# Layer 1's queries and forward forget gates, projected for pairs of heads ahead of the head loop by seven quarter products

## The chip, the cores and the metric

The kernel runs on one NeuronCore of a Trainium2 chip. The core has TensorE (PE, matmuls into PSUM banks; PEld are its weight loads), VectorE (DVE), ScalarE (ACT), GpSimd (POOL) and SyncE (SP, which here only issues DMAs), and 16 DMA engines between DRAM and SBUF. The metric is the device time of one execution in microseconds, taken as the median of several runs.

## The reference

Two layers work on 1024 latent tokens (`LAT`) and 256 context tokens (`CTX`) of width 1024. Layer 0 (attention and mLSTM heads) is not touched. Layer 1 has 16 heads of a gated linear recurrence that runs forward and backward:

```python
q, f_fwd, f_bwd, i, z = _split_cols(h @ w_in, C_SIZES)      # five blocks of 2048 columns
f = lb + (1.0 - lb) * jax.nn.sigmoid(f_pre.astype(F32))     # for each direction
k, lf, q = 1.0 - f, jnp.log(f), jax.nn.silu(q)
# per chunk: b = cumsum(lf);  S = exp(bL) * S + (k * exp(bL - b))^T v;  o = (q * exp(b)) S + ...
```

Each head takes 128 columns of each block. The queries are wanted for the latent tokens, the two forget gates `f_fwd` and `f_bwd` for latent and context tokens, the values `i` for both, the output gate `z` for the latent ones. The head outputs are normalised, multiplied by `silu(z)` and go through an output projection.

## The kernel before

The activations of layer 1 lie in SBUF transposed, as `hh + hl`: a value rounded to the matmul's 32-bit type and the rest. Weights are split the same way on arrival (`split`, L73 on ACT and L74 on DVE). `dense` (L131 to L133) makes each product from three matmuls, high by high, high by low, low by high, over k-blocks of 128 rows; a full projection of 128 columns has 8 k-blocks, so 24 matmuls for each group of up to 512 tokens.

Layer 1 handles the 16 heads one after the other, in this order of emission. `hg_proj` projects the forget gates of both directions (three token groups each: 256, 512, 512; sigmoid at L988, scaling at L989) into the tile `gF`, and the queries (two groups of 512, L997 and L998) into `gq`. `hg_intra` makes `k = 1 - f` (`gK`, L1061), two sums `gkn` (L1068), `Q = q * f` (`gQ`, L1070) and a first set of small matmuls ("strips", L1091), and then runs seven levels (`hg_level`): a copy of selected keys (`gksel`, L1121, ACT), 16 pairs of strips on PE, and on DVE `gQ` and `gK` times the decay (L1138), a masked copy (L1144) and the next level's decay (L1142). A level writes over the `gQ` that its strips read. `hg_vz` projects values and output gates (`wz` weights, 216 matmuls of 256 columns, outputs `gv` and `gz`). `hg_close` transposes `gK` (L1103, copies L1105), `hg_ctx` makes the state that the context leaves (L1043, L1045, L1050, L1052), `hg_scan` carries states backward (L1158, L1160) and forward (L1174, L1176) over 8 chunks and sums the output (L1169 to L1171). Then `hg_proj` of the next head is emitted, and the finished head goes out to DRAM.

The order on each engine is set by a planner that walks through the emitted instructions with its own idea of durations: an instruction that is ready and was emitted earlier goes first, the strips and the levels before all else (`urgent`). Each engine then works through its fixed order, and a semaphore holds an instruction whose inputs are late. `gQ`, `gK`, `gA`, `gz` and the `wz` weights have one buffer each; `gq` and `gv` have two; `gF` alternates between two pools from head to head. PSUM has two banks for projections (`mm`), two for transposes (`tr`), and three for strips and states (`s`). The next head's projections need neither this head's `gQ` nor its `gK`, so that they can lie anywhere in this head. After head 15 comes the output projection, whose first product is filled in during that head.

The lines that the change touches in `build` are these:

```python
wf = [self.wring([a["wc"][:, 2048 : 2048 + P]], P), None]   # weights of head 0, while layer 0 ends
st = self.hg_proj(0, pool, wf)
for h in range(16):
    hv = self.hg_intra(h, st, pool)
    self.hg_vz(h, st, pool)
```

## Time and profile before

| What | Value |
|---|---|
| Median of 3 runs | 3349.77 us (3348.98 to 3350.4) |
| Profiled execution, first to last instruction | 3349.2 us; its own time is not listed, the median lies 0.6 us above this span |
| PE busy in the span | 3316.9 us (99%) |
| DVE, ACT, POOL busy | 2028.9, 1401.3, 659.4 us (61%, 42%, 20%) |
| First key tile of a head (L1061) | head 0 at 1820.8 us, head 15 at 3120.3 us |
| Moved by DMA | 342.02 MB, mean 102 GB/s |

An engine's busy time is the union of its instructions. Matmuls overlap one another, and their ends are modelled, so that the time of a matmul in a stream is better read from the distance between two starts than from its duration. In a list of instructions in order of time, a bracket gives the idle time of the engine before the instruction, and what ended it. In a list of windows, each engine has its busy microseconds and the number of its instructions.

### The profile page before, as it was taken

The numbers are of one execution on the slowest core, as the hardware profiler recorded it, in microseconds if no ns is written. First come the engines' busy times: TensorE is split into PE (matmuls) and PEld (weight loads), VectorE is DVE, ScalarE is ACT, GpSimd is POOL, SyncE is SP. The second block draws the span as 40 slices with busy tenths as digits, with TensorE's granted clock in tenths as the row PEclk, the third lists the DMA queues.
The fourth block names the chain that finished last, engine by engine and source line by source line (L and its number), as shares of the span: only waits on it lengthen the run. The fifth ranks groups of instructions, "written<-read, shape, count | busy, mean of one in ns | idle before, by whom it ended". The sixth has DMA issues, their size and how long they took to land. (4 is left out here: it accounts for less than half of the span.)

```text
span 3349.2 us, 64282 instructions
## 1 busy us (share of the span) xinstructions
PE 3316.9 (99%) x25006; PEld 2940.9 (88%) x25006; DVE 2028.9 (61%) x4785; ACT 1401.3 (42%) x3301; POOL 659.4 (20%) x1059
## 2 busy tenths in 40 slices
PE   7999999999999999999999999999999999999999
PEld 6699899988989888898888999999999999999887
DVE  5337666666655466787666555555555555555657
ACT  5335554455443444454454333333333333333343
POOL 2222222212211111221110112121211222321110
PEclk9999999999999999999999999999999999999999
DMA  7713222232233444444653122211222222222267
GB/s 247 242 51 84 85 72 81 67 92 84 77 90 96 150 125 122 136 134 139 213 174 91 45 68 69 70 61 61 67 64 67 73 64 58 73 77 58 76 176 204
DMA packets 322992, 342.02 MB, mean 102 GB/s; under 512 B 32296, under 2 KB 265448, under 8 KB 321664
## 3 DMA queue, kind: packets, MB, share of 16 engines
q1 hardware_dynamic: 276816, 217.85, 22.3%
q0 software_dynamic: 45872, 120.07, 11.8%
q8 instruction: 197, 3.23, 0.4%
q14 instruction: 107, 0.88, 0.1%
HBM read 253.43 MB, written 84.21 MB: 101 GB/s over the span
## 5 line engine op out<-in xcount | busy, mean ns | idle before, releaser
L131 PE MATMUL mm<-hh,wh 128*128 128x512 f32 (+1 forms) x1600 | 585.4, 366 | 0.6 <-ACT gF L988 0.6
L132 PE MATMUL mm<-hl,wh 128*128 128x512 f32 (+1 forms) x1600 | 584.5, 365 | 0.0
L133 PE MATMUL mm<-hh,wl 128*128 128x512 f32 (+1 forms) x1600 | 580.6, 363 | 0.0
L131 PE MATMUL mm<-wh,hh 128*128 128x256 f32 (+1 forms) x1440 | 445.9, 310 | 1.7 <-DVE graw L1368 0.8
L132 PE MATMUL mm<-wl,hh 128*128 128x256 f32 (+1 forms) x1440 | 444.7, 309 | 0.0
L133 PE MATMUL mm<-wh,hl 128*128 128x256 f32 (+1 forms) x1440 | 442.0, 307 | 0.0
L131 PEld LDWEIGHTS mm<-hh,wh 128*128 128x128 f32 x1600 | 301.5, 188 | 47.6 <-ACT ev L371 4.2
L133 PEld LDWEIGHTS mm<-hh,wl 128*128 128x128 f32 x1600 | 301.5, 188 | 43.6 <-issue 0.2
L132 PEld LDWEIGHTS mm<-hl,wh 128*128 128x128 f32 x1600 | 301.7, 189 | 40.5 <-issue 0.2
L133 PE MATMUL mm<-wzh,hl 128*128 128x256 f32 x1024 | 291.6, 285 | 0.0
L132 PE MATMUL mm<-wzl,hh 128*128 128x256 f32 x1024 | 291.6, 285 | 0.0
L131 PE MATMUL mm<-wzh,hh 128*128 128x256 f32 x1024 | 291.3, 284 | 0.0
L131 PEld LDWEIGHTS mm<-wh,hh 128*128 128x128 f32 x1440 | 271.3, 188 | 20.7 <-ACT ev L352 3.4
L132 PEld LDWEIGHTS mm<-wl,hh 128*128 128x128 f32 x1440 | 271.4, 188 | 12.8 <-issue 0.7
L133 PEld LDWEIGHTS mm<-wh,hl 128*128 128x128 f32 x1440 | 271.3, 188 | 12.0 <-issue 0.5
L74 DVE TENSOR_TENSOR wl<-wraw,wh 128x512 fp32r<-128x512 f32 x240 | 165.8, 696 | 129.7 <-ACT wh L73 126.5
L73 ACT CAST wh<-wraw 128x512 fp32r<-128x512 f32 x240 | 147.2, 619 | 230.9 <-PE mm L132 181.6
L1121 ACT COPY gksel<-gK 128x1024 f32<-128x1024 f32 x96 | 111.0, 1156 | 224.5 <-PE s L1091 154.5
L132 PEld LDWEIGHTS mm<-wzl,hh 128*128 128x128 f32 x1024 | 193.5, 189 | 2.5
L131 PEld LDWEIGHTS mm<-wzh,hh 128*128 128x128 f32 x1024 | 193.2, 189 | 2.6
L133 PEld LDWEIGHTS mm<-wzh,hl 128*128 128x128 f32 x1024 | 193.3, 189 | 1.6
L1138 DVE TENSOR_TENSOR gQ<-gQ,gF 128x1024 f32<-128x1024 f32 x112 | 138.1, 1233 | 77.9 <-PE s L1091 77.9
(488 smaller groups left out, 7414.9 us busy)
## 6 DMA issues: line engine op xcount, KB each, us to landing
wraw<-in_wab_dram SPq DMA_DIRECT2D x108, 256.0 KB
wraw<-in_wc_dram SPq DMA_DIRECT2D x96, 256.0 KB
wraw<-yd SPq DMA_DIRECT2D x92, 256.0 KB
wraw<-in_wc_dram SPq DMA_DIRECT2D x128, 128.0 KB
md<-ev POOLq DMA_DIRECT2D x60, 256.0 KB, 2.7
mloz<-md SPq DMA_DIRECT2D x40, 256.0 KB
s<-gyt POOLq DMA_DIRECT2D x36, 256.0 KB, 4.4
adar<-in_wada_dram SPq DMA_DIRECT2D x16, 512.0 KB
```

The lines of the kernel that those rows point to most:

```text
L73: m = nc.scalar.copy(hi, x)
L74: nc.vector.tensor_tensor(out=lo, in0=x, in1=hi.bitcast(F32), op=ALU.subtract)
L131: mm(ps, lhsT=lh(k), rhs=rh(k), start=(start and k == 0), stop=False)
L132: mm(ps, lhsT=lh(k), rhs=rl(k), start=False, stop=False)
L133: m = mm(ps, lhsT=ll(k), rhs=rh(k), start=False, stop=(stop and k == nk - 1))
L1121: m = nc.scalar.copy(ksel.rearrange("p (b s i) -> p b s i", s=2, i=h), pick(K))
L1138: nc.vector.tensor_tensor(out=v, in0=v, in1=tot, op=ALU.mult)
```

## The change

`hg_f` keeps from the old `hg_proj` only the backward forget gate of a head. Queries and forward forget gates are made for all heads by `hg_wide`, which runs after layer 0 and after `hg_f` of head 0, and before the pool of the head loop is opened. It takes 16 units, queries and gates in turn for each pair of heads. A unit sees `h` (1024 tokens by 1024 features) and its 256 columns of W as two by two quarters of 512 tokens by 512 features and of 512 features by 128 columns, and makes the two by two result from seven products of quarters. `half_sums` makes four sums of quarters of `h` once; `raws` loads four weight quarters per unit and makes four differences on POOL. Each product has 4 k-blocks, so 12 matmuls of 512 columns. Partial sums are combined in PSUM and by DVE; results go through sigmoid and scaling as before, and to the DRAM scratches `qd` and `fd`. The gates' context tokens (`cpart`) have the same matmuls as before, with half of the k-blocks at a time. `hg_proj` now loads a head's queries and forward gates from DRAM with four DMAs on SP. The value and output-gate weights of head 0 are loaded at the end of `hg_wide`.

```diff
-    def dense(self, ps, lh, ll, rh, rl, nk, start=True, stop=True):
+    def dense(self, ps, lh, ll, rh, rl, nk, start=True, stop=True, skip=False):
...
-    def hg_proj(self, h, pool, w=None):
+    def hg_f(self, h, pool, w=None):
         nc, a = self.nc, self.a
-        st = {}
-        col = lambda i: a["wc"][:, i * 2048 + h * P : i * 2048 + (h + 1) * P]
+        c0 = 2 * 2048 + h * P
         lb, olb = self.lb[:, 0, h : h + 1], self.lb[:, 1, h : h + 1]
         fp = pool if h % 2 else self.fp
         F = self.t(fp, [P, 2, LAT], F32, "gF", 1)
         Fc = self.t(fp, [P, 2, CTX], F32, "gFc", 1)
-        todo = [(d, t0, n) for d in range(2) for t0, n in ((LAT, CTX), (512, 512), (0, 512))]
-        if w:
-
-            todo.sort(key=lambda x: x[1] == 0)
-        w = w or [None, None]
-        for d, t0, n in todo:
-            w[d] = w[d] or self.wring([col(1 + d)], P)
+        w = w or self.wring([a["wc"][:, c0 : c0 + P]], P)
+        for t0, n in ((LAT, CTX), (512, 512), (0, 512)):
             ps = self.ps("mm", [P, n])
-            self.proj_tr(ps, w[d], 0, t0, n)
-            dst = Fc[:, d, :] if t0 == LAT else F[:, d, t0 : t0 + 512]
+            self.proj_tr(ps, w, 0, t0, n)
+            dst = Fc[:, 1, :] if t0 == LAT else F[:, 1, t0 : t0 + 512]
             nc.scalar.activation(dst, ps, AF.Sigmoid)
             nc.vector.tensor_scalar(out=dst, in0=dst, scalar1=olb, scalar2=lb, op0=ALU.mult, op1=ALU.add)
+        return F, Fc
+    def hg_proj(self, h, pool, FF=None):
+        dma = self.nc.sync.dma_start
+        F, Fc = FF or self.hg_f(h, pool)
+        dma(out=F[:, 0, :], in_=self.fd[h, :, 0:LAT])
+        dma(out=Fc[:, 0, :], in_=self.fd[h, :, LAT:T])
         q = {}
-        w = self.wring([col(0)], P)
-        for t0 in (512, 0):
-            ps = self.ps("mm", [P, 512])
-            self.proj_tr(ps, w, 0, t0, 512)
-            q[t0 // 512] = self.t(pool, [P, 512], F32, "gq", 2)
-            sg = self.t(pool, [P, 512], F32, "gsg", 1)
-            nc.scalar.activation(sg, ps, AF.Sigmoid)
-            nc.vector.tensor_tensor(out=q[t0 // 512], in0=sg, in1=ps, op=ALU.mult)
+        for hf in (1, 0):
+            q[hf] = self.t(pool, [P, 512], F32, "gq", 2)
+            dma(out=q[hf], in_=self.qd[h, :, hf * 512 : hf * 512 + 512])
         return dict(F=F, Fc=Fc, q=q)
 
+    def half_sums(self, pool, tp):
+        nc = self.nc
+        hh, hl = self.hh, self.hl
+        S = {n: [self.t(pool, [P, 4, 512], F32R, f"st{n}{c}", 1) for c in "hl"] for n in range(1, 5)}
+        def A(t, c, j):
+            s = slice(512 * t, 512 * t + 512)
+            return hh[:, 4 * c + j, s].bitcast(F32), hl[:, 4 * c + j, s].bitcast(F32)
+        def done(n, j, x):
+            self.split(S[n][0][:, j, :], S[n][1][:, j, :], x)
+        def pair(eng, out, x, y, op):
+            e = self.t(tp, [P, 512], F32, "br", self.brs)
+            eng.tensor_tensor(out=out, in0=x[0], in1=y[0], op=op)
+            eng.tensor_tensor(out=e, in0=x[1], in1=y[1], op=op)
+            eng.tensor_tensor(out=out, in0=out, in1=e, op=ALU.add)
+        tt = nc.vector.tensor_tensor
+        s1 = []
+        for j in range(4):
+            s1.append(self.t(tp, [P, 512], F32, "br", self.brs))
+            pair(nc.vector, s1[j], A(1, 0, j), A(1, 1, j), ALU.add)
+            done(1, j, s1[j])
+        s3 = []
+        for j in range(2):
+            s3.append(self.t(tp, [P, 512], F32, "br", self.brs))
+            pair(nc.gpsimd, s3[j], A(0, 0, j), A(1, 0, j), ALU.subtract)
+        for j in range(4):
+            for x in A(0, 0, j):
+                tt(out=s1[j], in0=s1[j], in1=x, op=ALU.subtract)
+            done(2, j, s1[j])
+        for j in range(4):
+            if j > 1:
+                s3.append(self.t(tp, [P, 512], F32, "br", self.brs))
+                pair(nc.gpsimd, s3[j], A(0, 0, j), A(1, 0, j), ALU.subtract)
+            done(3, j, s3[j])
+        for j in range(4):
+            h, l = A(0, 1, j)
+            tt(out=s1[j], in0=h, in1=s1[j], op=ALU.subtract)
+            tt(out=s1[j], in0=s1[j], in1=l, op=ALU.add)
+            done(4, j, s1[j])
+        return S
+    def hg_wide(self, sp, tp):
+        nc, a = self.nc, self.a
+        hh, hl = self.hh, self.hl
+        self.brs = 10
+        S = self.half_sums(sp, tp)
+        add = lambda out, x, y: nc.vector.tensor_tensor(out=out, in0=x, in1=y, op=ALU.add)
+        def X(n):
+            if isinstance(n, int):
+                return [lambda k, t=t: t[:, k, :] for t in S[n]]
+            t, c = n
+            return [lambda k, x=x: x[:, 4 * c + k, 512 * t : 512 * t + 512] for x in (hh, hl)]
+        def prod(ps, w, n, first):
+            x = X(n)
+            self.dense(ps, w.h, w.l, x[0], x[1], 4, first, True, True)
+        def raws(kind, i):
+            c0 = (2048 if kind == "f" else 0) + 2 * i * P
+            b = {}
+            for r, c in ((0, 0), (0, 1), (1, 1), (1, 0)):
+                b[(r, c)] = self.t(tp, [P, 512], F32, "br", self.brs)
+                nc.sync.dma_start(
+                    out=b[(r, c)].rearrange("p (k f) -> p k f", f=P),
+                    in_=a["wc"][r * 512 : r * 512 + 512, c0 + c * P : c0 + c * P + P].rearrange("(k p) f -> p k f", p=P),
+                )
+            def sub(x, y, out=None):
+                o = self.t(tp, [P, 512], F32, "br", self.brs) if out is None else out
+                nc.gpsimd.tensor_tensor(out=o, in0=x, in1=y, op=ALU.subtract)
+                return o
+            b["t1"] = sub(b[(0, 1)], b[(0, 0)])
+            b["t2"] = sub(b[(1, 1)], b["t1"])
+            b["t3"] = sub(b[(1, 1)], b[(0, 1)], None if kind == "f" else b[(0, 1)])
+            b["t4"] = sub(b[(1, 0)], b["t2"])
+            return b
+        units = [(kind, i) for i in range(8) for kind in "qf"]
+        order = lambda kind: [(0, 0), "t2", (1, 0), "t3", "t1", "t4"] + ([(0, 1)] if kind == "f" else []) + [(1, 1)]
+        queue = [(u, n) for u in range(len(units)) for n in order(units[u][0])]
+        rawd, forms = {}, {}
+        def more(n):
+            for u, f in queue[:n]:
+                if u not in rawd:
+                    rawd[u] = raws(*units[u])
+                hi, lo = [self.t(self.wp, [P, 512], F32R, "w" + c, self.slabs) for c in "hl"]
+                self.split(hi, lo, rawd[u][f])
+                forms[(u, f)] = _W([hi], [lo], 4, P)
+            del queue[:n]
+        more(3)
+        for u, (kind, i) in enumerate(units):
+            def form(n):
+                more(1)
+                return forms.pop((u, n))
+            def finish(t, c, x):
+                h = 2 * i + c
+                o = self.t(tp, [P, 512], F32, "co", 2)
+                nc.scalar.activation(o, x, AF.Sigmoid)
+                if kind == "q":
+                    nc.vector.tensor_tensor(out=o, in0=o, in1=x, op=ALU.mult)
+                else:
+                    nc.vector.tensor_scalar(
+                        out=o, in0=o, scalar1=self.lb[:, 1, h : h + 1], scalar2=self.lb[:, 0, h : h + 1],
+                        op0=ALU.mult, op1=ALU.add,
+                    )
+                d = self.qd if kind == "q" else self.fd
+                nc.gpsimd.dma_start(out=d[h, :, 512 * t : 512 * t + 512], in_=o)
+            def tail(t, c, ps, x):
+                o = self.t(tp, [P, 512], F32, "ct", 2)
+                add(o, ps, x)
+                finish(t, c, o)
+            ctx = {}
+            def cpart(c, w, k0, stop):
+                if kind == "q":
+                    return
+                if c not in ctx:
+                    ctx[c] = self.ps("tr", [P, CTX])
+                self.dense(
+                    ctx[c], w.h, w.l, lambda k: hh[:, k0 + k, LAT:T], lambda k: hl[:, k0 + k, LAT:T], 4, not stop, stop
+                )
+                if stop:
+                    h = 2 * i + c
+                    o = self.t(tp, [P, 512], F32, "co", 2)[:, 0:CTX]
+                    nc.scalar.activation(o, ctx[c], AF.Sigmoid)
+                    nc.vector.tensor_scalar(
+                        out=o, in0=o, scalar1=self.lb[:, 1, h : h + 1], scalar2=self.lb[:, 0, h : h + 1],
+                        op0=ALU.mult, op1=ALU.add,
+                    )
+                    nc.gpsimd.dma_start(out=self.fd[h, :, LAT:T], in_=o)
+            p1, u2, u3 = [self.t(tp, [P, 512], F32, n, 1) for n in ("p1", "u2", "u3")]
+            pa, pb, pc = self.ps("mm", [P, 512]), self.ps("x", [P, 512]), self.ps("x", [P, 512])
+            w = form((0, 0))
+            prod(pa, w, (0, 0), True)
+            nc.scalar.copy(p1, pa)
+            cpart(0, w, 0, False)
+            prod(pb, form("t2"), 2, True)
+            add(u2, pb, p1)
+            w = form((1, 0))
+            prod(pa, w, (0, 1), False)
+            finish(0, 0, pa)
+            cpart(0, w, 4, True)
+            prod(pb, form("t3"), 3, False)
+            add(u3, pb, p1)
+            prod(pc, form("t1"), 1, True)
+            tail(1, 1, pc, u3)
+            prod(pb, form("t4"), (1, 1), False)
+            tail(1, 0, pb, p1)
+            if kind == "f":
+                cpart(1, form((0, 1)), 0, False)
+            w = form((1, 1))
+            prod(pc, w, 4, False)
+            tail(0, 1, pc, u2)
+            cpart(1, w, 4, True)
-    def hg_vz(self, h, st, pool):
+    def hg_vz(self, h, st, pool, w=None):
         nc, a = self.nc, self.a
         col = lambda i: a["wc"][:, i * 2048 + h * P : i * 2048 + (h + 1) * P]
-        w = self.wblock(pool, "wz", [col(3), col(4)], KD, 256)
+        w = w or self.wblock(pool, "wz", [col(3), col(4)], KD, 256)
...
+            self.qd = self.scratch(dr, "qd", [16, P, LAT])
+            self.fd = self.scratch(dr, "fd", [16, P, T])
...
-                        wf = [self.wring([a["wc"][:, 2048 : 2048 + P]], P), None]
+                        wf = self.wring([a["wc"][:, 4096 : 4096 + P]], P)
...
-                wf[1] = self.wring([a["wc"][:, 4096 : 4096 + P]], P)
 
             with l1:
+                FF = self.hg_f(0, None, wf)
+                with tc.tile_pool(name="st", bufs=1) as sp, tc.tile_pool(name="sx", bufs=1) as tp, self.pp.phase(x=4):
+                    self.hg_wide(sp, tp)
+                    col = lambda i: a["wc"][:, i * 2048 : i * 2048 + P]
+                    wv = self.wblock(
+                        self.wp, "w", [col(3), col(4)], KD, 256, [tp, self.brs, "br"], ring=self.slabs
+                    )
                 pool = l1.enter_context(tc.tile_pool(name="hg", bufs=2))
                 self.rawp = pool
                 banks = l1.enter_context(ExitStack())
                 banks.enter_context(self.pp.phase(s=3, acc=1))
                 last = None
-                st = self.hg_proj(0, pool, wf)
+                st = self.hg_proj(0, pool, FF)
                 for h in range(16):
                     hv = self.hg_intra(h, st, pool)
-                    self.hg_vz(h, st, pool)
+                    self.hg_vz(h, st, pool, None if h else wv)
...
```

More of the change, by code (lines that the diff above doesn't have):

```diff
@@ L126, in behind @@
         )
-    def dense(self, ps, lh, ll, rh, rl, nk, start=True, stop=True):
+    def dense(self, ps, lh, ll, rh, rl, nk, start=True, stop=True, skip=False):
         mm = self.nc.tensor.matmul
         for k in range(nk):
-            mm(ps, lhsT=lh(k), rhs=rh(k), start=(start and k == 0), stop=False)
-            mm(ps, lhsT=lh(k), rhs=rl(k), start=False, stop=False)
-            m = mm(ps, lhsT=ll(k), rhs=rh(k), start=False, stop=(stop and k == nk - 1))
+            mm(ps, lhsT=lh(k), rhs=rh(k), start=(start and k == 0), stop=False, skip_group_check=skip)
+            mm(ps, lhsT=lh(k), rhs=rl(k), start=False, stop=False, skip_group_check=skip)
+            m = mm(ps, lhsT=ll(k), rhs=rh(k), start=False, stop=(stop and k == nk - 1), skip_group_check=skip)
         return m
```

## The prediction

> **What bounds the kernel now.** I read the page first (PE busy for 99% of the span), then PE's waits, then the windows and groups of one head in the middle of layer 1, and last its instructions in order of time.
>
> PE's waits, the largest one and the only one in the head loop above 0.2 us:
>
> ```profile
> PE ad L237 <- DMA adar<-in_wada_dram: 15.7, 5, 13.8
> ...
> PE tr L1103 <- DVE gK L1138: 0.4, 1, 0.4
> ```
>
> The key tile of all heads, and the windows of one head (microseconds and counts for PE, PEld, DVE, ACT, POOL, then the granted clock, the DMA share and GB/s):
>
> ```profile
> L1061 DVE TENSOR_SCALAR gK<-gF x16: 1215/1227/1883, 1820.8 to 3120.3; 128x2048 f32<-128x2048 f32 x16
> 2158.90:2246.30 87.40, 87.40 (x780) 79.57 (x780) 50.55 (x82) 29.20 (x61) 18.30 (x27) 1.00 0.21 67
> ```
>
> PE waits for nobody in the loop; DVE is busy for 50.6 of 87.4 us of a head. So today a head lasts as long as PE's list of work. What PE does in that head:
>
> ```profile
> L132 PE MATMUL mm<-hl,wh 128*128 128x512 f32 x49 | 19.5, 397 | 0.0
> L132 PE MATMUL mm<-wzl,hh 128*128 128x256 f32 x64 | 18.3, 286 | 0.0
> ...
> L1091 PE MATMUL s<-gQ,gksel 128*64 128x64 f32 x192 | 7.4, 231 | 0.0
> L132 PE MATMUL mm<-hl,wh 128*128 128x256 f32 x16 | 4.7, 294 | 0.0
> ```
>
> Each projection row is one of three alike, so 144 matmuls of 512 (six groups of 24; one of the 49 belongs to a neighbour), and 192 and 48 of 256, with 24 more of 256 for the context's values by the code. The distance between starts, over 15 matmuls of 512 and over 27 of 256:
>
> ```profile
> 2232.61 0.40 PE L131 MATMUL mm<-hh,wh 128*128 128x512 f32 x1
> ...
> 2236.04 0.39 PE L131 MATMUL mm<-hh,wh 128*128 128x512 f32 x1
> ...
> 2286.70 0.28 PE L131 MATMUL mm<-wzh,hh 128*128 128x256 f32 x1
> ...
> 2289.88 0.28 PE L131 MATMUL mm<-wzh,hh 128*128 128x256 f32 x1
> ```
>
> 3.43/15 = 0.229 us and 3.18/27 = 0.118 us. The projections of a head, which I call fill since they wait for nothing in it, are 144 x 0.229 + 264 x 0.118 = 64.1 us. The other 87.4 - 64.1 = 23.3 us are the recurrence's own matmuls with the changes between kinds.
>
> **Removed and added on PE.** Each head loses two groups of 512 for q, and two of 512 and one of 256 for the forward gate: 96 x 0.229 + 24 x 0.118 = 24.8 us, 397 us for 16 heads. Added are 16 units of seven products of 12 matmuls, 84 x 0.229 = 19.2 us each, and 48 matmuls of 256 for the context in each of 8 gate units, 5.7 us: 308 + 45 = 353 us. The balance is -44 us, if PE is full in both places.
>
> **Is PE full in the new stage?** Splits of weights cost as much as elsewhere; POOL's differences are nearest to L1218, which has two tile inputs of this size:
>
> ```profile
> L74 DVE TENSOR_TENSOR wl<-wraw,wh 128x512 fp32r<-128x512 f32 x240 | 165.8, 696 | 129.7 <-ACT wh L73 126.5
> ...
> L1218 POOL TENSOR_TENSOR gknc<-gEc,gknc x8: 1270/1534/1751, 1993.5 to 2607.0; 128x512 f32<-128x512 f32 x8
> ...
> DMA packets 322992, 342.02 MB, mean 102 GB/s; under 512 B 32296, under 2 KB 265448, under 8 KB 321664
> ```
>
> A query unit has 7 splits, 5 sums with PSUM and 4 last products, 16 x 0.69 = 11.0 us on DVE; POOL has 4 x 1.53 = 6.1 us, and 4 DMA issues. A gate unit is similar, with 25 us of PE to hide it. So both lie beside PE's 19.2 us, and the splits run three products (8 us) ahead. I cost this at nothing. A unit moves some 2 MB in 19 us, 105 GB/s, no more than the kernel's mean (102 GB/s), so that DMA isn't the bound either. Were each difference to stall PE once, it would cost 6.1 x 16 = 98 us, the upper bound.
>
> The start isn't hidden. Layer 0's last output matmul, and the last piece of `h`:
>
> ```profile
> 1788.74 0.40 PE L925 MATMUL mm<-wh,yl 128*128 128x512 f32 x1
> ...
> 1803.49 0.29 DVE L318 TENSOR_TENSOR hl<-ntmp,hh 128x128 fp32r<-128x128 f32 x1 [0.17 <-ACT hh L317]
> ```
>
> In these 14.8 us PE now works ahead on head 0's gates. Only the backward one is left, 24 x 0.118 + 24 x 0.229 = 8.3 us before the last tokens are wanted: 6 us idle. Then 5.5 us of its last group and 2.7 us of the first product stand against the second product's input, the second sum: 12 DVE instructions at 0.69, 8.3 us, if the first sum is done by then, else 28, 19.3 us, and 11 us more of idle time. Bounds 6 and 17 us; I take 12, as nothing shows when the new pools' memory comes free.
>
> The Trainium skill speaks against POOL's share ("SBUF — State Buffer", section "SBUF: two separate sides"): VectorE and GpSimd hold their shared ports exclusively, and a DVE instruction in a two-port mode or with two SBUF inputs blocks for the length of a POOL one. The trace agrees for one kind:
>
> ```profile
> L1038 DVE TENSOR_SCALAR gq<-gFc x16: 427/1124/1125, 1831.9 to 3142.1; 128x512 f32<-128x512 f32 x16
> ```
>
> It takes 0.43 us, or 1.12 us where a POOL product lies beside it. By that rule the six POOL instructions beside the first sums, 6 x 1.53 = 9 us, would come on top of the start; a unit's 11.0 + 6.1 us would still fit.
>
> **What the head loop does with less fill.** This decides. The four stretches of a head, by instructions of DVE, ACT and PE in order of time:
>
> ```profile
> 2188.74 1.23 DVE L1138 TENSOR_TENSOR gQ<-gQ,gF 128x1024 f32<-128x1024 f32 x1 [1.12 <-PE s L1091]
> ...
> 2222.28 1.22 DVE L1138 TENSOR_TENSOR gQ<-gQ,gF 128x1024 f32<-128x1024 f32 x1
> 2223.42 1.22 DVE L1138 TENSOR_TENSOR gK<-gK,gF 128x1024 f32<-128x1024 f32 x1
> ...
> 2228.27 1.07 ACT L1105 COPY gkn<-tr 128x512 f32<-128x512 f32 x2
> ...
> 2231.27 1.03 PE L1103 MATMUL tr<-ident,gK 128*128 128x128 f32 x8
> ...
> 2231.91 1.07 ACT L1105 COPY gkn<-tr 128x512 f32<-128x512 f32 x2 [0.28 <-PE tr L1103]
> ...
> 2236.72 0.60 PE L1043 MATMUL tr<-ident,gq 128*128 128x128 f32 x4
> 2237.36 0.59 ACT L1045 COPY gknc<-tr 128x512 f32<-128x512 f32 x1 [4.38 <-PE tr L1043]
> 2242.17 1.05 PE L1050 MATMUL s<-gv,gknc 128*128 128x128 f32 x8
> ...
> 2243.65 0.35 DVE L1160 SCALAR_TENSOR_TENSOR gS<-gS,gT,s 128x128 f32<-128x128 f32 x1
> ...
> 2257.33 0.35 DVE L1176 SCALAR_TENSOR_TENSOR gS<-gS,gT,s 128x128 f32<-128x128 f32 x1 [0.97 <-PE s L1174]
> ...
> 2276.08 1.23 DVE L1138 TENSOR_TENSOR gQ<-gQ,gF 128x1024 f32<-128x1024 f32 x1 [1.12 <-PE s L1091]
> ```
>
> Levels 33.5 us (2188.7 to 2222.3), closing and context 21.4, backward scan 13.7, forward scan to the next head's first level 18.8: 87.4 together. Between its steps the recurrence stands behind fill: L1045 ends at 2237.95, and L1050, which needs only it, starts 4.2 us later, with PE at fill all the while. Without fill I estimate each stretch from its own rows:
>
> ```profile
> L1138 DVE TENSOR_TENSOR gQ<-gQ,gF 128x1024 f32<-128x1024 f32 x7 | 8.6, 1224 | 4.2 <-PE s L1091 4.2
> L1138 DVE TENSOR_TENSOR gK<-gK,gF 128x1024 f32<-128x1024 f32 x7 | 8.5, 1220 | 0.3
> ...
> L1144 DVE COPY_PREDICATED gD<-glm,s 128x512 f32<-128x512 uint8 x6 | 4.4, 737 | 0.0
> ...
> L1142 DVE TENSOR_TENSOR gF<-gF x96: 173/340/1215, 1837.2 to 3182.1; 128x1024 f32<-128x1024 f32 x16, 128x512 f32<-128x512 f32 x16, 128x256 f32<-128x256 f32 x16, 128x128 f32<-128x128 f32 x16
> ```
>
> Levels: DVE needs 8.6 + 8.5 + 4.4 + 3 (L1142, halving from 1.2) = 24.5 us for seven, 21 for six. Closing and context: 2.4 (last L1138 pair) + 0.5 + 1.07 + 1.03 + 1.07 + 0.6 + 0.59 + 1.05 + 0.6 us, with eight hand-overs, about 10. Backward scan: seven times 0.35 us and the next keys, about 5.5. Forward scan: PE's own some 8 us and the new `gQ`, about 10.5. Together 47 us, less than the 62.6 us of PE work left (87.4 - 24.8). So a full PE is possible. But the fill left is 39.3 us for stretches that now take up 64.1, and the planner puts fill in whenever it is ready. The output gates' fill becomes ready when `gz` is free, after the forward scan, so the levels keep their 33.5 - 7.4 = 26 us of it (7.4 are the strips), and 13.3 us are left for the closing stretch, which takes 18.1 today (21.4 less 3.3 of its own matmuls, L1103, L1043 and L1050). Its bare rest is 10 x 4.8/18.1 = 2.7 us, and the two scans are left bare. A head then is 33.5 + 13.3 + 3.3 + 2.7 + 5.5 + 10.5 = 68.8 us, 6.2 above 62.6. If the loss spread evenly, it would be 47 + 40.4 x 39.3/64.1 = 71.8, 9.2 above; if the levels were bare, 21 + 21.4 + 13.7 + 18.8 = 74.9, 12.3 above. I take 7.5 us, between the first two, since the trace shows no head with less fill. 15 heads hold a next head's projections: 112 us.
>
> The four loads per head (1.1 MB) join SP's queue ahead of the `wz` weights; the `gq` buffers they wait for come free with this head's L1043, a whole backward scan before the next `gQ`. I cost them at nothing; were they late, the next head's L1070 would be, by a DMA's length. ACT and DVE lose the sigmoids and splits, off the path.
>
> **Sum.** 3349.2 - 44 + 12 + 112 = 3429 us of span, and 0.6 us to the median: 3430. Its own range, with 4.5 to 10 us of idle time per head and 6 to 17 at the start, is 3379 to 3473.
>
> **Rivals.** *PE stays full in the loop* (chance 0.28): 3349.8 - 44 + 6 to 17, so 3312 to 3323. For it: 47 us of recurrence against 62.6 us of work; against: fill is spent early, and each hand-over then shows. It turns into a loss at 2.1 us of idle time per head, (44 - 12)/15. *The levels are left bare* (0.16): 12.3 us per head, 3349.8 - 44 + 12 + 185 = 3503; DVE's 4.2 us of waiting for strips with fill about speaks against it. *The seven products take as long as eight* (0.08), held by POOL and the splits: 98 us on top of the forecast, 3528, or 3416 on a full PE. The forecast has 0.48.
>
> A measurement of this kernel can tell about 0.2% (6.7 us) from no change. Faster: 0.28, and 0.01 of the forecast's edge; same (idle 1.7 to 2.6 us per head): 0.05; slower: 0.66. The range 3314 to 3500 leaves out half of the bare levels, most of the stage's rival and the fastest of the full PE, about 0.2.
>
> **What would show it.** Heads (L1061 to L1061) of 68 to 72 us, with PE waits on L1158, L1171 and L1043 that are absent now; a stage of 353 to 375 us before them; PE's waits at its start, 6 to 17 us, on DVE. Heads of 63 us would prove me wrong, heads of 75 us would move the loss to the levels; and a stage above 390 us would mean that products don't follow at 0.229 us.

## The result and the profile after

Four executions of the changed kernel take 3419.45 to 3431.52 us, median 3423.22; the kernel before, beside it, 3349.93. The ratio is 1.0225 with a 95% interval of 1.021 to 1.0239, so the change makes the kernel slower by 2.2%, 73 us. The profiled execution took 3423.08 us with a span of 3421.3.

Three marks cut the span: the last matmul of layer 0's output, and the first and last key tile. These are the last matmul of L925 in PE's order of time (start and duration), and the key tile's group among its groups of instructions (least, median and longest in ns, first and last start).

```profile
1789.35 0.40 PE L925 MATMUL mm<-wh,yl 128*128 128x512 f32 x1
```

```profile
L1226 DVE TENSOR_SCALAR gK<-gF x16: 1226/1227/1229, 2199.9 to 3199.3; 128x2048 f32<-128x2048 f32 x16
```

Up to the first mark little moved (1789.35, before 1788.74). From there to head 0's keys it takes 410.6 us, before 32.1: 378.5 more. From head 0's keys to head 15's it takes 999.4 us, before 1299.5: 300.1 less. From there to the end it takes 222.0, before 228.9: 6.9 less. The sum is 71.5 us, and 0.6 come from layer 0: the 72.1 by which the span grew.

The first part has its loss at the beginning. These are windows of PE, PEld, DVE, ACT and POOL (busy microseconds and counts), then the granted clock:

```profile
1790.00:1800.00 10.00, 8.37 (x46) 6.83 (x45) 8.80 (x22) 4.50 (x13) 1.34 (x3) 1.00 0.06 26
1800.00:1810.00 10.00, 7.80 (x27) 5.05 (x27) 9.35 (x17) 4.44 (x15) 7.40 (x6) 0.83 0.00 0
1810.00:1820.00 10.00, 2.01 (x7) 0.78 (x5) 9.27 (x7) 3.18 (x6) 9.61 (x7) 0.77 0.10 29
1820.00:1830.00 10.00, 2.04 (x4) 1.23 (x5) 10.00 (x18) 4.55 (x8) 2.00 (x1) 0.50 0.28 79
1830.00:1840.00 10.00, 4.55 (x12) 2.77 (x11) 6.85 (x10) 3.47 (x7) 9.23 (x4) 0.67 0.00 1
1840.00:1850.00 10.00, 10.00 (x32) 7.90 (x33) 9.24 (x11) 3.21 (x6) 6.25 (x4) 0.70 0.39 113
1850.00:1900.00 50.00, 50.00 (x243) 41.97 (x242) 27.70 (x41) 16.97 (x29) 17.14 (x19) 1.00 0.37 117
```

From 1800 to 1840 PE is busy for 16.4 of 40 us, and the clock falls to half. DVE is busy for 35.5 of the same 40. From 1850 on PE is full at clock 1.00, with DVE at 55% and POOL at a third.

PE's waits of the whole execution, without the one at the kernel's beginning:

```profile
PE mm L131 <- ACT wh L73: 12.5, 2, 12.2
PE acc L1334 <- DVE gA L1354: 9.4, 15, 0.7
PE s L1256 <- DVE gQ L1235: 7.7, 10, 0.9
PE acc L1335 <- DVE gS L1325: 6.7, 15, 0.7
PE s L1323 <- DVE gS L1325: 5.5, 15, 0.4
PE x L131 <- ACT wh L73: 5.4, 2, 3.9
PE s L1256 <- DVE gS L1341: 3.5, 13, 0.6
PE mm L133 <- DVE wl L74: 3.1, 1, 3.1
```

The single long waits (12.2, 3.9, 3.1) belong to the start. Those that occur 10 to 15 times, at most once in a head, belong to the two scans and to the next head's first strips. Before the change the head loop had none above 0.4 us.

One head in the middle, by DVE's rows in order of time: `gQ` of the first level, `gQ` of the last level, the first state of the backward scan, the first of the forward scan, `gQ` of the next head's first level.

```profile
2681.90 1.22 DVE L1303 TENSOR_TENSOR gQ<-gQ,gF 128x1024 f32<-128x1024 f32 x1
...
2714.75 1.22 DVE L1303 TENSOR_TENSOR gQ<-gQ,gF 128x1024 f32<-128x1024 f32 x1
...
2732.84 0.35 DVE L1325 SCALAR_TENSOR_TENSOR gS<-gS,gT,s 128x128 f32<-128x128 f32 x1
...
2737.51 0.33 DVE L1341 SCALAR_TENSOR_TENSOR gS<-gS,gT,s 128x128 f32<-128x128 f32 x1
...
2749.96 1.23 DVE L1303 TENSOR_TENSOR gQ<-gQ,gF 128x1024 f32<-128x1024 f32 x1
```

Levels 32.9 us (before 33.5), closing and context 18.1 (21.4), backward scan 4.7 (13.7), forward scan 12.4 (18.8): 68.1 together, before 87.4. Counted by its matmuls' starts, at the prediction's 0.229 and 0.118 us, the fill left in this head is 24.2 us in the levels, 14.4 in the closing, 0.7 in the backward scan and none in the forward scan; in the head of the prediction it was 25.2, 17.9, 11.9 and 9.1. The levels have kept nearly all of theirs, and both scans have lost theirs.

For the comparison of runs I leave out head 0, part of whose values is made ahead. The second key tile stands at 2254.72 us, so that the other heads take (3199.3 - 2254.72)/14 = 67.5 us. Before, (3120.3 - 1898.2)/14 = 87.3; less the 24.8 us of matmuls removed, a full PE would need 62.5. The loop loses 5.0 us a head.

Not all of this is idle time of PE. These are the windows of 14 heads, after and before, in the columns as above:

```profile
2254.72:3199.30 944.58, 908.88 (x9197) 834.71 (x9196) 639.34 (x1013) 341.14 (x735) 277.71 (x382) 1.00 0.30 88
```

```profile
1898.24:3120.28 1222.04, 1221.02 (x10880) 1111.45 (x10879) 707.31 (x1131) 410.50 (x856) 257.39 (x372) 1.00 0.23 66
```

PE is idle for 35.7 us, 2.6 a head; before it was 0.1. The other 2.4 us count as busy. The 28 matmuls of a head that make the scans' states (L1323 and L1339, before L1158 and L1174) start 0.17 us apart in the mean, waits left out, and 0.08 before: 2.6 us a head. Whether PE works or waits in that time the profile doesn't tell, since the ends of matmuls are modelled; the list of waits has none of it.

### The profile page after: what moved, and what is told of

Read it like the earlier page. It is cut to its first block, busy times and chain, and to the rows that moved or that the text cites. A ratio compares the mean times of both kernels' runs of the same rounds, so it can differ in the third digit from the quotient of the medians.

```text
span 3421.3 us, 64930 instructions
## 1 busy us (share of the span) xinstructions
PE 3324.6 (97%) x24814; PEld 2927.6 (86%) x24814; DVE 2186.1 (64%) x4965; ACT 1454.6 (43%) x3389; POOL 834.7 (24%) x1215
## 5 line engine op out<-in xcount | busy, mean ns | idle before, releaser
L131 PE MATMUL mm<-wh,hh 128*128 128x256 f32 (+1 forms) x1504 | 464.2, 309 | 1.9 <-DVE graw L1535 0.7
L132 PE MATMUL mm<-wl,hh 128*128 128x256 f32 (+1 forms) x1504 | 462.9, 308 | 0.0
L131 PE MATMUL mm<-hh,wh 128*128 128x512 f32 (+1 forms) x1096 | 400.3, 365 | 12.8 <-ACT wh L73 12.2
L133 PE MATMUL mm<-hh,wl 128*128 128x512 f32 (+1 forms) x1096 | 396.1, 362 | 3.1 <-DVE wl L74 3.1
L132 PE MATMUL mm<-hl,wh 128*128 128x512 f32 (+1 forms) x1096 | 396.9, 362 | 1.6 <-DVE hl L318 1.6
L131 PEld LDWEIGHTS mm<-hh,wh 128*128 128x128 f32 x1096 | 207.5, 189 | 47.9 <-ACT wh L73 12.6
L133 PEld LDWEIGHTS mm<-hh,wl 128*128 128x128 f32 x1096 | 207.2, 189 | 33.8 <-DVE wl L74 3.8
L132 PEld LDWEIGHTS mm<-hl,wh 128*128 128x128 f32 x1096 | 207.5, 189 | 31.9 <-DVE hl L318 4.3
L74 DVE TENSOR_TENSOR wl<-wraw,wh 128x512 fp32r<-128x512 f32 x176 | 120.0, 689 | 77.9 <-ACT wh L73 75.4
L1303 DVE TENSOR_TENSOR gK<-gK,gF 128x1024 f32<-128x1024 f32 x112 | 143.0, 1276 | 5.3 <-DVE gF L1307 0.5
```

Of the source, the lines that this page charges most:

```text
L74: nc.vector.tensor_tensor(out=lo, in0=x, in1=hi.bitcast(F32), op=ALU.subtract)
L131: mm(ps, lhsT=lh(k), rhs=rh(k), start=(start and k == 0), stop=False, skip_group_check=skip)
L132: mm(ps, lhsT=lh(k), rhs=rl(k), start=False, stop=False, skip_group_check=skip)
L133: m = mm(ps, lhsT=ll(k), rhs=rh(k), start=False, stop=(stop and k == nk - 1), skip_group_check=skip)
L1303: nc.vector.tensor_tensor(out=v, in0=v, in1=tot, op=ALU.mult)
```

## The experiments

Each run gives the 95% interval of its ratio to the kernel before, which took 3348.2 to 3349.6 us beside them. The stage is measured in the traces as above, from layer 0's last matmul to head 0's keys; in the four traces whose start is that of the changed kernel it takes 409.2 to 410.6 us.

### What the start costs, and why

*Eight plain products* in place of seven, with no sums of `h` and no differences of weights, and buffers of its own for the first unit's weights:

```diff
-        S = self.half_sums(sp, tp)
+        plain = lambda kind, i: True
...
+                for c in range(2):
+                    pp = [self.ps("x", [P, 512]) for _ in range(2)]
+                    for r in range(2):
+                        w = form((r, c))
+                        for t in (1, 0):
+                            prod(pp[t], w, (t, r), r == 0)
```

> All 16 units take eight plain products, without sums of h or differences of weights; the place of the work, the results in DRAM and the head loop stay. By matmuls alone the stage is 16 x 12 x 0.229 = 44 us longer. Theory: the seven products themselves run at 0.23 us a matmul and so save these 44 us, but their start costs some 30 us more than that of plain products: 3428 to 3444 us. If the sevens' splits and differences also slow the rest of the stage, less: below 3425. If plain products have the same start, 3460 us or more.

Measured: 3432.71 us (1.0231 to 1.0262), as the theory had it. Layer 0's last matmul and the key tile, in the same two views of this run:

```profile
1788.96 0.40 PE L925 MATMUL mm<-wh,yl 128*128 128x512 f32 x1
```

```profile
L1243 DVE TENSOR_SCALAR gK<-gF x16: 1226/1227/1230, 2209.7 to 3209.0; 128x2048 f32<-128x2048 f32 x16
```

The stage takes 420.7 us, 10.2 more than with seven products, where the matmuls alone are 44 more. So the seven products save their 44 us, and 34 of them go into a start that the plain products don't have. PE waits there once for 1.8 us and once for 0.5, so the change's start costs some 36 us in all, in place of the 12 in the prediction. A count by the starts of PE's matmuls in the changed kernel, from 1789.75 to 1850 us, agrees: 25.2 us of idle time, and 10.2 us by which the matmuls there take longer than 0.229 (512 columns), 0.118 (256) and 0.107 us (128); 39 of the 94 with 512 columns start over 0.35 us apart. In the same stretch the plain products have 2.3 and 0.5 us. The loop is the same: (3209.0 - 2263.2)/14 = 67.6 us a head.

*Buffers of its own for the first unit's weights*, which are loaded and split ahead of the sums. In the changed kernel, SP's load of these weights waits 18.6 us for POOL to free a buffer of `br` (`buf` gives the first unit the tiles `u2`, `u3`, `ct`, `co` and `p1`, and all others the ring `br`):

```diff
-                b[(r, c)] = self.t(tp, [P, 512], F32, "br", self.brs)
+                b[(r, c)] = buf((r, c))
...
-        S = self.half_sums(sp, tp)
...
         more(3)
+        S = self.half_sums(sp, tp)
```

> The first unit's four weight quarters and their differences get buffers of their own, and are loaded and split ahead of the sums of h; all else stays. Theory: at the start of the new stage the first weights stand behind the sums, because both take their buffers from one ring (br), and so PE waits 12.2 us for wh. Then the first product follows the backward gate's last matmul at once, the waits on wh (12.2 and 3.9 us) and wl (3.1) go, a wait of some 8 us for the second sum st2 stays, and the matmuls at half clock become fewer: the start costs 14 to 18 us in place of 35.6, the time is 3402 to 3406 us. Rival: DVE, with the last pieces of h and the sums, sets the start anyway; then the wait only moves from wh to st2 and the time is 3415 to 3423 us.

Measured: 3421.76 us (1.0205 to 1.0235), the rival's answer. PE's waits from 1790 to 1860 us, of this run:

```profile
PE x L131 <- ACT st2h L73: 9.3, 1, 9.3
PE tr L294 <- DVE nx L282: 6.3, 1, 6.3
PE x L132 <- DVE st2l L74: 3.2, 1, 3.2
```

The waits for `wh` are gone, but now PE waits for the second sum, and for `nx`, the last norm, which DVE reaches only after sums and weight splits. The stage is only 5.5 us shorter (first keys at 2191.4, layer 0's last matmul at 1786.34). The ring caused the wait that the list named, but DVE, busy for 47.6 of the 50 us from 1790 to 1840, set the end.

*The third sum on DVE in place of POOL*, and then *both edits*:

```diff
-            pair(nc.gpsimd, s3[j], A(0, 0, j), A(1, 0, j), ALU.subtract)
+            pair(nc.vector, s3[j], A(0, 0, j), A(1, 0, j), ALU.subtract)
```

> The third sum's differences are made on DVE in place of POOL; all else stays. Theory: POOL's instructions beside the last pieces of h hold up DVE (L318 takes 1.1 us in place of 0.28), so that the backward gate's last group and the sums end about 8 us later than they could. Then L318 stays at 0.28 us, the last piece of h is written near 1804 in place of 1811.9, and the time falls by 5 to 8 us, to 3415 to 3418, since the first weights still stand behind the sums. Rival: the weights alone set the start; then the last pieces come earlier and PE waits for wh as much longer: 3421 to 3425 us, or 2 to 4 us more, as DVE has 12 more instructions of 0.69 us.

> The two edits together: own buffers for the first unit's weights, and all sums on DVE. If ring and port are the two causes of the long start, it costs 8 to 14 us (one wait for st2 stays) and the time is 3396 to 3402 us. If the ring alone counts, 3402 to 3406 as with the first edit; if the sums on DVE are the limit, no better than 3410.

Measured: 3416.18 us (1.0188 to 1.0218) and 3417.74 (1.0185 to 1.022); the stages are 9.4 and 10.5 us shorter. The one group of L318 from 1803 to 1813 us in the changed kernel, and one of this line's instructions in the run without POOL's sums:

```profile
L318 DVE TENSOR_TENSOR hl<-ntmp,hh x7: 1043/1133/1371, 1803.0 to 1810.5; 128x128 fp32r<-128x128 f32 x7
```

```profile
1808.71 0.29 DVE L318 TENSOR_TENSOR hl<-ntmp,hh 128x128 fp32r<-128x128 f32 x1
```

The last seven pieces of `h` took 1.1 us each beside POOL's sums and take 0.29 without. This is the port rule that the prediction weighed. The stage gained 9.4 us, though DVE got 12 instructions more; but in this pair of runs the ring's buffers may come free earlier as well. Where the first unit's weights don't use the ring, the same edit gains 5.0 us (405.1 to 400.1) and, with the plain first unit below, 10.4 (395.4 to 385.0). So POOL beside DVE is shown as a cause, with 5 to 10 us. The expectation had the size in the time right (3415 to 3418) but not the last piece, which comes at 1808.7 and not at 1804, since the sums now stand among the pieces. The two edits together gain no more than the one, against the expectation: 3417.7 lies in the range of neither cause but in that of "no better than 3410", DVE.

*A plain first unit*: eight products for the first unit only, from its own buffers and ahead of the sums, so that PE has 22 us of work that needs no sum. Then *the same with all sums on DVE*:

```diff
+        plain = lambda kind, i: (kind, i) == ("q", 0)
...
```

> The first of the 16 units (queries of heads 0 and 1) takes eight plain products, which need no sums of h, from buffers of its own, ahead of all sums; the other 15 stay. Theory: the long start (35.6 us) is DVE's 40 and more instructions for the sums behind the last piece of h, with PE idle and then at a lower clock. With 22 us of products to run meanwhile, PE doesn't idle long, the clock stays at 1.0, and the start costs 4 to 12 us, 2.75 of them for the eighth products: 3391 to 3402 us. Rival: it's rather the weights' way (loads, splits, POOL beside DVE), which this unit needs too: then 3410 us or more.

> The plain first unit together with all sums on DVE. In the run with the plain first unit a last piece of h still took up to 5.1 us on DVE in place of 0.29, beside POOL's sums. Theory: DVE and POOL on one port pair are what is left of the start; without POOL's sums it falls from about 18 us to 8 to 12 and the time from 3413.7 to 3403 to 3408 us. Rival: DVE's own list of sums is what is left, and 12 more of 0.69 us on it take back what the port gives: 3410 to 3418 us.

Measured: 3413.73 us (1.0176 to 1.0212) and 3406.08 (1.015 to 1.0184). The first falls to the rival, and of the rival's causes it is POOL beside DVE: one of the last pieces of `h` takes as long as four of POOL's instructions:

```profile
1804.23 5.12 DVE L318 TENSOR_TENSOR hl<-ntmp,hh 128x128 fp32r<-128x128 f32 x1
```

In the second, PE is nearly full through the start and the clock stays. These are its windows, in the columns as above, and its key tile:

```profile
1800.00:1810.00 10.00, 9.51 (x46) 7.45 (x45) 7.40 (x18) 5.62 (x17) 1.36 (x3) 1.00 0.13 54
1810.00:1820.00 10.00, 8.78 (x39) 6.93 (x38) 9.88 (x22) 5.61 (x13) 0.00 (x0) 1.00 0.19 53
1820.00:1830.00 10.00, 10.00 (x47) 8.32 (x46) 10.00 (x15) 5.21 (x11) 4.95 (x3) 1.00 0.18 52
```

```profile
L1244 DVE TENSOR_SCALAR gK<-gF x16: 1226/1227/1229, 2174.2 to 3183.6; 128x2048 f32<-128x2048 f32 x16
```

DVE is as busy as in the changed kernel, but now something lies beside it. The stage takes 385.0 us (layer 0's last matmul at 1789.19), 25.6 less, with 2.75 more of products: the start has fallen from 36 to 8 us. The time falls by only 17, since in this execution the loop took 10 us more; six of its heads ran at a granted clock of 0.98, against one at 0.97 in the change's. The run with both edits differs from this one in the first unit alone, and the stage goes from 400.1 to 385.0 us, 17.9 less when its 2.75 us of products are left out. So of the 36 us the two edits take away 10.5 (own buffers alone 5.5, the sums on DVE alone 9.4; they overlap), work for PE beside DVE's sums takes away 17.9 more, and 8 are left.

### What the head loop loses, and why

*The output gate in two halves* with three buffers, so that the next head's projections may start in this head's scans:

```diff
-        z = self.t(pool, [P, NT - 2, P], F32, "gz", 1)
+        z = [self.t(pool, [P, 4, P], F32, "gz", 3) for _ in range(2)]
...
-            s = self.t(pool, [P, P], F32, "gS1", 10)
+            s = self.t(pool, [P, P], F32, "gS1", 8)
...
```

> The output gate tile gz is cut into two halves with three buffers in place of one whole tile, so that the next head's value and gate projections may start during this head's scans (the backward states gS1 have 8 buffers in place of 10, for the room). Theory: the head loop loses some 5 us per head because its fill is spent when the scans come, and the next fill waits for gz. Then 15 to 24 matmuls or more of fill stand in the scans, a head takes 62.5 to 63.5 us in place of 66.6, and the time is 3361 to 3378 us. Rival: the loss is the recurrence's own hand-overs, which fill on the same engine can't hide, or fill is only moved from the levels, which then wait: a head stays at 66 us or more and the time at 3413 to 3425 us.

Measured: 3469.56 us (1.0348 to 1.0379), 46 us worse than the change, outside both expectations. The key tile, and three windows from one head's scans:

```profile
L1226 DVE TENSOR_SCALAR gK<-gF x16: 1219/1221/1229, 2195.9 to 3240.7; 128x2048 f32<-128x2048 f32 x16
```

```profile
2750.00:2755.00 5.00, 3.44 (x25) 2.86 (x23) 4.32 (x9) 0.66 (x2) 3.30 (x5) 1.00 0.19 63
2755.00:2760.00 5.00, 3.94 (x19) 3.88 (x19) 1.76 (x4) 0.00 (x0) 2.96 (x5) 0.52 0.39 131
2760.00:2765.00 5.00, 4.14 (x50) 3.88 (x50) 3.24 (x7) 1.47 (x8) 0.97 (x3) 0.80 0.01 3
```

A head takes 70.7 us in place of 67.5 (second key tile at 2250.9). By the marks above, the four stretches of the head with these windows are 32.8, 13.3, 5.8 and 19.6 us: the closing is 5 us shorter than in the change, the forward scan 7 us longer. Some fill did move into the scans, but not to where it was wanted: the last of it stands among the backward states, PE has no fill from 2751.3 to 2766.3 us, and 4.5 us of it stand in the scan's end. Three waits of 0.92, 0.64 and 1.06 us in the gap are followed by matmuls at half clock. The backward states also had two buffers less here, and this run doesn't separate the two edits.

*A higher priority for closing and scans* in the planner, and the same with the plain first unit:

```diff
+                    with self.urgent():
                         self.hg_close(hv, pool)
                         S = self.hg_ctx(st, pool)
                         self.hg_scan(st, hv, S, pool)
```

> The closing transposes, the context's states and both scans of a head get the planner's priority that the strips and levels have, ahead of all projections; nothing else changes. Theory: a head is a chain of levels (32 us, with room for 26 us of fill), closing and two scans, and fill that was emitted earlier stands ahead of the closing (20 us between the last strips and the first backward state, where the bare steps need about 10), so that none is left for the scans. Then the closing shortens, its fill moves into the scans' waits, a head takes 63 to 65.5 us in place of 67.4 and the time is 3365 to 3395 us. Rival: fill is short however it is ordered, since the levels can't take less and the scans' steps follow each other on PE and DVE; a head stays at 66.5 us or more and the time is 3410 to 3430 us.

> The priority for closing and scans together with the plain first unit. The two act in different places, so their gains add up: by the theories 3335 to 3372 us, which is the before's 3348 give or take; by the rivals no better than 3400.

Measured: 3426.04 us (1.021 to 1.0244) and 3413.87 (1.0177 to 1.0208), which are the change and the plain first unit again. From the second head on, PE's order is the same as in the changed kernel, matmul by matmul, so this says nothing on the theory: presumably those instructions weren't ready earlier by the planner's own durations. The next run forces the order.

*The value and gate projections held* until the first backward state (`self.hold` is the first matmul of L1323 in the head before):

```diff
+            if k == 0 and self.hold:
+                self.behind(m0, self.hold)
...
```

> The next head's value and gate projections (72 matmuls of 256 that now run in the closing) are held on PE until this head's first backward state; nothing else changes. Theory: in the closing the transposes and the context's states stand behind this fill (gK is final at 2717.0, its first transpose comes at 2720.4; gknc is copied at 2729.0, its reader comes at 2731.35), while the scans after it are bare. Moved by 8.6 us of work, the fill covers the scans' waits and the closing shortens by 4 to 6 us: a head takes 63 to 65.5 us in place of 67.4, the time is 3365 to 3398 us. Rival: the closing's own hand-overs then show instead, and the backward states stand behind fill: a head stays at 66.5 us or more, the time at 3410 to 3430 us.

Measured: 3435.12 us (1.024 to 1.0271), the rival. PE's waits in the loop:

```profile
PE acc L1339 <- ACT gA L1317: 14.1, 14, 2.1
PE tr L1271 <- DVE gK L1306: 11.2, 14, 1.4
PE acc L1339 <- DVE gA L1359: 11.1, 8, 1.7
PE s L1218 <- ACT gknc L1213: 9.4, 14, 0.7
```

The waits have left the scans' states (L1323 and L1335 of the changed kernel) and stand in the closing, on `gA` by ACT, `gK` and `gknc`, and in the second half of the forward scan, on `gA` by DVE. By the same marks as above, the medians of 11 heads are 34.6 us of levels, 8.0 of closing, 8.9 of backward and 16.5 of forward scan; the closing is 10 us shorter, all else longer, and a head takes 68.4 us. So moving the fill didn't pay: there is too little of it for all gaps.

*Queries alone ahead* (with the plain first unit), the forward gates in the heads as before; then *the hold* added:

```diff
-        units = [(kind, i) for i in range(8) for kind in "qf"]
+        units = [(kind, i) for i in range(8) for kind in "q"]
...
```

> Only the queries are made ahead (8 units, the first with eight plain products); the forward gates are projected in the heads again, as before the change. By matmuls alone that is 22 us less than before, 2.75 more for the first unit, and a start that has head 0's gates and a plain unit beside the sums (3 to 6 us). Theory: the loop loses because fill is short; with 50 us of fill a head in place of 39, against 64 before, it loses 0 to 2 us a head, so 76.3 to 78.3 us a head, and the time is 3334 to 3364 us, at the low end faster than before. Rival: the loss isn't the amount of fill but loads and order around it; then some 5 us a head stay and the time is 3400 us or more.

> Queries alone ahead, as in the run beside it, and the value and gate projections held until the first backward state. If the loop is full with 50 us of fill, this changes nothing (within 5 us of the run beside it); if some idle time is left in the scans, it gains 5 to 20 us; if the hold itself costs (backward states behind fill, bare closing), it loses 5 to 20 us.

Measured: 3386.49 us (1.0093 to 1.0127) and 3379.77 (1.0076 to 1.0106). The key tiles of the two, whose second ones stand at 2053.58 and 2053.20 us:

```profile
L1246 DVE TENSOR_SCALAR gK<-gF x16: 1219/1227/1230, 1992.3 to 3160.6; 128x2048 f32<-128x2048 f32 x16
```

```profile
L1249 DVE TENSOR_SCALAR gK<-gF x16: 1226/1227/1229, 1991.9 to 3153.8; 128x2048 f32<-128x2048 f32 x16
```

A head takes 79.1 us, and 78.6 with the hold; a full PE would need 87.3 - 48 x 0.229 = 76.3. The time lies between the two expectations. The start has PE's waits of 8 us in place of 3 to 6, 6.3 of them for one split. The loop's loss is 2.8 us, more than the theory's 0 to 2 and less than the rival's 5. With 11.0 us of fill taken out (53.1 are left, not the 50 of the expectation) 2.8 come back, 1.6 of them as idle PE; with 24.8 us 5.0, 2.6 of them idle. With this much fill the hold gains 0.5 us a head, 7 us in the time, the second of its three cases.

No version tried beats the kernel before. The best of them, at 3379.77 us, is still 0.9% slower.

## Why the prediction was right, and where it was not

The forecast was 3430 us and slower; 3423 was measured. The direction and both mechanisms held, lost fill in the loop and an uncovered start. That the total lies only 7 us from the forecast is luck: two terms were mis-sized in opposite senses and cancel, the start at 36 us for 12 and the loop at some 79 for 112 (of the 71.5 us after layer 0, 397 are removed, 353 added and 36 the start; 79.5 are left, for the loop with its two ends).

- *PE's balance of -44 us*: held. From 1850 us on PE is full at clock 1.00, and with eight products the stage is 44 us longer less what the start gives back. The rival that seven take as long as eight is out. (Its price of 98 us was that of POOL holding up PE at each difference; eight products for seven are 44.) The sign that a stage above 390 us would mean products not following at 0.229 us was ill chosen: the stage took 410.6, and yet its matmuls of 512 start 0.231 us apart in the mean from 1862 to 2185 us. The start was 24 us longer, and by these marks 14 us of the heads' work fall into the stage (378.5 us more, less 353, less 36, and the 24.8 that head 0 lost), such as head 0's values.
- *DVE and POOL beside the products at nothing*: held once the stage runs; POOL's differences took 1.535 us in the mean, as taken from L1218 (1.534). The splits became slower, 0.795 us for 0.696, and from 1850 us on that was covered.

```profile
L1072 POOL TENSOR_TENSOR br<-br,br 128x512 f32<-128x512 f32 x64 | 98.1, 1535 | 53.2 <-DVE wl L74 34.0 <-DVE st3l L74 8.3 <-DMA br<-in_wc_dram 4.1
L74 DVE TENSOR_TENSOR wl<-br,wh 128x512 fp32r<-128x512 f32 x124 | 97.3, 795 | 28.7 <-ACT wh L73 27.5
```

- *The start at 12 us, 6 to 17*: wrong, and this is the step that failed. It set the backward gate's last group and the first product against 12 DVE instructions, and took the first product's weights and the pieces of `h` to be in time. The weights stood in one ring of buffers with the sums; with that undone, DVE was still late. Of the causes, POOL beside DVE is shown (5 to 10 us), and that DVE's sums with nothing on PE to cover them are most of the rest is shown by the plain first unit (17.9 us, with 8 left). Of the 36 us, 25 are idle PE and at most 10 are the lower clock; in the run with the plain first unit and all sums on DVE, where PE hardly waits, it stays at 1.00. The rule of the Trainium skill ("SBUF — State Buffer", section "SBUF: two separate sides"), which the prediction put beside its own term as 9 us more, was borne out in kind: with it the start would have been forecast at 21 us, still 15 short. That its 9 us are near the 9.4 gained is in part luck, since 12 of POOL's instructions, not six, stood beside DVE's.
- *Idle time in the loop, 7.5 us a head*: right in place, too large, and only half of it idle. The fill went where the prediction had put it, 24.2 us in the levels (26) and 14.4 in the closing (13.3), and the scans are bare; but of the 5.0 us that a head loses, 2.6 are idle PE, and the rest lies between the scans' state matmuls and counts as busy, which the term didn't have. The stretches by themselves were 33.5, 19.3, 5.5 and 10.5 us, 68.8 together; the head above has 32.9, 18.1, 4.7 and 12.4, 68.1. The mis-sized term is the mean with the even spread (71.8), which I had no row for; the first estimate alone was within 1.3 us of the 67.5 measured.
- *Where it shows*: heads take 67.5 us, just under the 68 to 72 that were named. Of the three lines named for PE's new waits, L1158 (now L1323) has them; L1171 and L1043 (L1336, L1208) have none. In their place stand L1335, L1334 on `gA`, and the next head's strips (L1256) on `gQ`: the same scans, other hand-overs. Levels stayed as they were, so the rival of bare levels (75 us a head) is out, and so is the full PE (62.6).
- *Four loads per head at nothing*: held; after head 0, where `gQ` waits 1.2 us for `gq`, no engine's list of waits in the loop has `gq` or `gF` waiting for a DMA.

## What to carry to other kernels

A saving of matmuls taken out of a loop is also fill taken out of it: here a fifth to a quarter of the time removed from each head came back (2.8 of 11.0, 5.0 of 24.8), about half of it as idle time and the rest as longer distances between small matmuls, which count as busy; and moving the remaining fill around won back at most 0.5 us a head. A new stage has to be priced at its beginning, with every engine's work that must come before its first product; some independent products put there were worth more than mending the wait that the profile named. And when two terms of a sum are uncertain, check them one by one in the result, since a total that fits says little about either.

## What the runs showed of the hardware that I had not expected

*TensorE's clock after short waits.* The same head, in the same order and with the same wait of 0.57 us before the forward scan's first L1335, in the changed kernel and in the run with the higher priority, as windows (bounds, length, busy time of PE, PEld, DVE, ACT and POOL, granted clock):

```profile
2657.96:2725.38 67.42, 64.74 (x660) 59.58 (x659) 44.88 (x73) 24.13 (x53) 19.53 (x27) 1.00 0.28 89
```

```profile
2658.35:2727.94 69.59, 66.43 (x660) 61.20 (x659) 45.64 (x73) 24.16 (x53) 19.27 (x27) 0.98 0.27 86
...
2669.00:2674.00 5.00, 4.43 (x22) 3.93 (x22) 3.48 (x8) 0.00 (x0) 4.75 (x7) 0.70 0.14 48
```

In the second the clock fell to 0.70 over 5 us of the scans, and the head is 2.2 us longer. This happens in some heads and not in others: with the same order of matmuls from the second head on, five heads of the second run lie at 0.97 or 0.98 and one in the first, and the second's loop is 4.8 us longer. It is likely, but not shown, as only one execution has a trace, that this is why the changed kernel's executions lie 12 us apart, at mean clocks of 0.992 to 0.996, while those of the kernel before, at 1.00, lie 1.4 us apart. The Trainium skill ("TensorE: Matmul & The Clock Gate", section "Why this matters for your kernels") asks for no idle gap above some 3 us, and tells elsewhere ("A second HAM failure mode: psum-queue depth-cycling") of a kernel whose frequent short idle times let the clock swing, without their length. Here the waits before the fall were 0.37 and 0.57 us, among small matmuls, and the other run had the same two waits without a fall; what decides between them stays open.

*DVE beside POOL.* A DVE instruction of 0.29 us with two SBUF inputs took 1.1 us beside one POOL instruction, and once 5.12 us beside four in a row: it did not get its turn between them. These are POOL's rows beside the 5.12 us from 1804.23, in the run with the plain first unit:

```profile
1804.21 1.31 POOL L1013 TENSOR_TENSOR br<-hl 128x512 f32<-128x512 f32 x1
1805.47 1.29 POOL L1012 TENSOR_TENSOR br<-hh 128x512 f32<-128x512 f32 x1
1806.71 1.26 POOL L1013 TENSOR_TENSOR br<-hl 128x512 f32<-128x512 f32 x1
1807.93 1.25 POOL L1012 TENSOR_TENSOR br<-hh 128x512 f32<-128x512 f32 x1
```

POOL pays too: in the changed kernel four of L1072 in a row took 11.31 us, 2.8 each, while DVE's sums ran, and one took 1.36 us a little later.

```profile
1828.00 11.31 POOL L1072 TENSOR_TENSOR br<-br,br 128x512 f32<-128x512 f32 x4 [8.31 <-DVE st3l L74]
...
1843.25 1.36 POOL L1072 TENSOR_TENSOR br<-br,br 128x512 f32<-128x512 f32 x1 [3.94 <-DMA br<-in_wc_dram]
```
